# The S5 mixer of a recurrent decoder step: state operators by selection products on TensorE in place of products on VectorE and GpSimd

## The chip, the cores and the metric

The kernel runs on one core of a Trainium2 chip. The metric is the device time of one execution in microseconds (us); lower is better. The engines are TensorE (PE in the profile, its weight loads PEld), VectorE (DVE), ScalarE (ACT), GpSimd (POOL) and SyncE (SP, which here only issues DMAs).

## What is computed

One step of a decoder trunk on 592 tokens (16 meta tokens and a prompt of 512, then 8 running sequences of 8 tokens each), all in float32: an S5 layer, a causal convolutional feed-forward (ConvFFN), an RG-LRU layer, a second ConvFFN, each with a residual and a layer norm. The change is in the S5 layer. It projects x (592 x 1024) to u, runs 64 groups of 16 channels through a diagonal complex state space of 64 states a group, applies GELU, and multiplies by the output weights with a gate (GLU). For a group the recurrence is

```
A    = exp(step * lam)                  # 64 complex numbers
Bbar = (A - 1) / lam * B                # 64 x 16
h[t] = A * h[t-1] + Bbar u[t]
y[t] = 2 Re(C h[t]) + D u[t]            # gelu(y) goes on
```

The kernel does it in chunks of 8 tokens: 74 chunks (66 of the prompt, one a sequence). In a chunk, y is a Toeplitz product of u with the lag operators C A^d Bbar, d = 0 to 7; the state that a chunk adds is a product of u with A^j Bbar, j = 0 to 7; the states go from chunk to chunk by a scan; and what a chunk gets from earlier ones is a product of the state with C A^d, d = 1 to 8.

## The kernel before

Four pairs of groups make a **quad** (8 groups, one tile of 128 channels); there are eight quads. Every quad passes through these functions:

- project(m, h): half h of the tokens of channel tile m of u, 24 products (three for each k tile, L155 to L157: high and low parts of both factors); fetch_u brings u back by group and chunk through DRAM (DMA ud, u).
- fetch(q): one DMA (bc, L461) brings B and C of the quad, two steps ahead of their use.
- inputs(q, r): the operators A^j Bbar, real (r = 0) or imaginary, on VectorE: two products and a sum over 128x512 (L473 to L475). flip(q, r): their four transposes on TensorE (L483), a copy on ScalarE (L485), two small ones (L488).
- carries(q, r): C A^d by two products of 128x1024 on GpSimd (L509) and a sum on VectorE (L513); carry0 (L499) stacks C.
- lags(q): the lag operators on TensorE (L524). windows(q): ScalarE and VectorE put them into one tile (L530, L531), which a DMA writes to DRAM (td, L535). fetch_lags(q): reads them back in Toeplitz form (lagged, L539); toeplitz(q) reorders them on ScalarE (toe, L544).
- states(q): the states each chunk adds, 16 products (L563), then turned back by the angle of the chunk on VectorE (L567 to L570) and summed on GpSimd (L577, L578). decays (L551) makes the decay row. scans(q): the two scans (L587), four products (L588 to L593), and four quarter sums on GpSimd (L597). ends(q) saves and replaces the last states.
- phases(a), tables(a): angles (VectorE L436 to L445) and their cosines and sines (ScalarE L453) of two quads.
- outputs(q, h): for each group the Toeplitz product (L614) and the product with the state (L615) into one PSUM tile, GELU (L617), the write to DRAM (gd). fetch_gy and split_gy bring it back as the factor of the GLU.

The order of the work is written by hand under manual_schedule: each engine does its instructions in the order of the calls, and each DMA queue in the order of its issues. A step s runs the operators of quad s + 1, the states, lags and scans of quad s and the outputs of quad s - 1, with halves of projections between. Weights are streamed by load (wraw), split by convert_hi on ScalarE (whi, L126) and convert_lo (wlo, L135), which in the S5 stage stands on GpSimd. Behind the S5 stage the GLU, the feed-forwards and the RG-LRU follow; the change leaves them as they are.

## Time and profile before

| | us |
|---|---|
| three timed runs | 1405.79, 1408.65, 1410.70 |
| median | 1408.65 |
| span of the profiled execution (first to last instruction) | 1403.4 |
| its last product of an S5 output (line L615) ends at | 209.4 |
| TensorE busy over the span | 1310.7 |
| VectorE busy over the span | 897.2 |

The profiled execution is another one than the three timed; its span leaves out what lies before the first and behind the last instruction. TensorE carries the program; its granted clock has a mean of 0.964 of full speed over the span.

### The profile page before, as it was taken

Reading aid. Unit: us, or ns where it says so; the run is one execution under the profiler, and the core shown is the slowest. Engines: PE = TensorE matmul, PEld = TensorE weight load, DVE = VectorE, ACT = ScalarE, POOL = GpSimd, SP = SyncE. Lnnn points to the kernel's source line nnn. Section 1 sums busy time; section 2 is a strip of 40 time slices with the busy share of each in tenths; the row PEclk is TensorE's granted clock in tenths of the full one; section 3 lists DMA queues with packets and bytes.
Section 4 is the critical chain, followed back from the end, with each engine's and each line's share of the span. In section 5 each row is a group of like instructions: output and inputs, shape, how many; then the busy total and the mean of one; then the engine's idle time right before and its main releaser. Section 6 shows DMA issues by size and latency. Waiting matters only on the chain.

```text
span 1403.4 us, 23686 instructions
## 1 busy us (share of the span) xinstructions
PE 1310.7 (93%) x9708; PEld 1287.2 (92%) x9708; DVE 897.2 (64%) x1455; ACT 591.5 (42%) x950; POOL 385.7 (27%) x392
## 2 busy tenths in 40 slices
PE   5668889998999999999998999998999999999995
PEld 4667779998999999999998999998999999999994
DVE  8999996358655345535547989839755245535546
ACT  3654464235433134313334587734434133313433
POOL 5667753247000000000027521167200000000036
PEclk9888679999999999999999999999999999999998
DMA  6255454211222222222221212221322222222211
GB/s 200 63 154 163 133 152 173 90 61 55 96 90 76 82 84 72 79 91 76 82 81 61 81 55 94 80 84 57 109 91 76 91 76 87 70 101 78 80 52 68
DMA packets 70989, 127.80 MB, mean 91 GB/s; under 512 B 21216, under 2 KB 42848, under 8 KB 70880
## 3 DMA queue, kind: packets, MB, share of 16 engines
q1 hardware_dynamic: 61120, 120.71, 26.2%
q10 hardware_dynamic: 9760, 5.57, 1.4%
q8 instruction: 76, 1.25, 0.4%
q14 instruction: 33, 0.27, 0.1%
HBM read 113.61 MB, written 12.66 MB: 90 GB/s over the span
## 4 chain that ended last, share of the span: by engine, by line
PE 72%; DVE 21%; ACT 2%; issue 2%; DMA 1%; POOL 0%; SPq 0%; DVEq 0%; ACTq 0%
PE mm L157 23%; PE mm L156 23%; PE mm L155 23%; DVE wb L474 2%; DVE res L898 2%; DVE lo L904 1%; DVE wz L473 1%; DVE wz L475 1%; DVE wlo L135 1%; DVE res L870 1%; DVE t L587 1%; DMA wraw<-in_w5i 1%; PE y L615 1%; DVE ph L440 1%; PE y L614 1%
## 5 line engine op out<-in xcount | busy, mean ns | idle before, releaser
L156 PE MATMUL mm<-lo,whi 128*128 128x296 f32 (+2 forms) x2800 | 839.4, 300 | 20.8 <-DVE lo L904 10.4
L155 PE MATMUL mm<-hi,whi 128*128 128x296 f32 (+2 forms) x2800 | 841.2, 300 | 12.7 <-ACT whi L126 7.2
L157 PE MATMUL mm<-hi,wlo 128*128 128x296 f32 (+2 forms) x2800 | 837.8, 299 | 1.7 <-DVE wlo L135 1.7
L156 PEld LDWEIGHTS mm<-lo,whi 128*128 128x128 f32 x2800 | 532.2, 190 | 28.0 <-DVE lo L904 15.5
L155 PEld LDWEIGHTS mm<-hi,whi 128*128 128x128 f32 x2800 | 532.4, 190 | 15.9 <-ACT whi L126 7.2
L157 PEld LDWEIGHTS mm<-hi,wlo 128*128 128x128 f32 x2800 | 531.4, 190 | 2.5 <-DVE wlo L135 2.5
L135 DVE TENSOR_TENSOR wlo<-wraw,whi 128x1024 fp32r<-128x1024 f32 (+1 forms) x172 | 214.2, 1250 | 212.9 <-ACT whi L126 212.2
L126 ACT ACTIVATE whi<-wraw 128x1024 fp32r<-128x1024 f32 (+1 forms) x188 | 194.4, 1039 | 305.1 <-PE mm L156 298.0
L1088 POOL TENSOR_TENSOR tmp<-tmp,hist 128x16 f32<-128x16 f32 x88 | 20.4, 234 | 697.5 <-DVE tmp L1085 697.5
L1083 DVE SCALAR_TENSOR_TENSOR tmp<-mm,sm,tmp 128x512 f32<-128x512 f32 (+2 forms) x176 | 131.9, 750 | 0.0
L1087 ACT ACTIVATE stg<-mm 128x18 f32<-128x18 f32 x88 | 16.3, 185 | 185.7 <-DVE tmp L1085 185.7
L1135 DVE TENSOR_TENSOR res<-mm,res 128x296 f32<-128x296 f32 (+3 forms) x48 | 25.9, 558 | 81.2 <-PE mm L157 81.2
L1078 ACT ACTIVATE tmp<-mm,sm 128x592 f32<-128x592 f32 (+1 forms) x88 | 72.1, 822 | 0.0
L831 POOL TENSOR_TENSOR s<-s,res 128x296 f32<-128x296 f32 (+2 forms) x45 | 42.7, 951 | 62.0 <-DVE res L1039 31.5
L1094 DVE TENSOR_TENSOR tmp<-tmp 128x592 f32<-128x592 f32 (+1 forms) x44 | 33.7, 766 | 38.7 <-ACT tmp L1093 38.7
L172 DVE TENSOR_TENSOR lo<-tmp,hi 128x592 fp32r<-128x592 f32 (+2 forms) x48 | 36.6, 763 | 27.3 <-ACT hi L171 27.3
L171 ACT ACTIVATE hi<-tmp 128x592 fp32r<-128x592 f32 (+2 forms) x48 | 33.1, 690 | 42.7 <-DVE tmp L1094 30.0
L927 POOL TENSOR_SCALAR res<-res,sm 128x592 f32<-128x592 f32 (+1 forms) x24 | 49.1, 2063 | 7.0 <-DVE lo L904 7.0
L135 POOL TENSOR_TENSOR wlo<-wraw,whi 128x1024 fp32r<-128x1024 f32 x16 | 45.4, 2840 | 20.5 <-ACT whi L126 20.4
L614 PE MATMUL y<-u,toe 128*128 128x74 f32 x128 | 36.0, 379 | 15.8 <-ACT toe L544 15.8
L1133 DVE SCALAR_TENSOR_TENSOR res<-res,mm 128x592 f32<-128x592 f32 (+1 forms) x16 | 12.2, 762 | 59.2 <-PE mm L157 59.2
L832 POOL TENSOR_TENSOR s<-s,tmp 128x296 f32<-128x296 f32 (+2 forms) x53 | 49.5, 938 | 0.3 <-ACT tmp L827 0.3
(276 smaller groups left out, 1412.0 us busy)
## 6 DMA issues: line engine op xcount, KB each, us to landing
wraw<-in_wup SPq DMA_DIRECT2D x88, 512.0 KB, 3.2
wraw<-in_wdn SPq DMA_DIRECT2D x32, 448.0 KB, 3.3
wraw<-in_w5o SPq DMA_DIRECT2D x16, 512.0 KB, 4.3
wraw<-in_wdn SPq DMA_DIRECT2D x16, 512.0 KB, 3.4
wraw<-in_wri SPq DMA_DIRECT2D x16, 512.0 KB, 3.6
wraw<-in_w5i SPq DMA_DIRECT2D x8, 512.0 KB, 5.2
td<-lagsb SPq DMA_DIRECT2D x8, 512.0 KB, 3.3
lagged<-td SPq DMA_DIRECT2D x8, 512.0 KB, 3.8
```

Of the source, the lines that this page charges most:

```text
L126: A.activation(hi[:, 0:kk, :], t[:, 0:kk, :], AF.Copy)
L135: eng.tensor_tensor(lo[:, 0:kk, :], t[:, 0:kk, :], hi[:, 0:kk, :].bitcast(F32), op=ALU.subtract)
L155: T.matmul(out, hi[:, k, :], xh, start=start, stop=False)
L156: T.matmul(out, hi[:, k, :], xl, start=False, stop=False)
L157: T.matmul(out, lo[:, k, :], xh, start=False, stop=stop)
L172: V.tensor_tensor(lo[:, scols], src[:, scols], hi[:, scols].bitcast(F32), op=ALU.subtract)
L614: T.matmul(out, toe[:, g, :], u[:, g, :], start=True, stop=False)
L831: G.tensor_tensor(self.s1[:, cs_], RES[0][:, cs_] if m == 1 else self.s1[:, cs_], z, op=ALU.add)
L832: G.tensor_tensor(self.s2[:, cs_], self.s2[:, cs_], sq[:, cs_], op=ALU.add)
L927: G.tensor_scalar(z, z, bm, None, op0=ALU.add)
L1078: A.activation(acc[:, d0:NT], X(d0, NT), AF.Identity, scale=w[2], bias=fcb[:, l, m:m + 1])
L1083: V.scalar_tensor_tensor(acc[:, a:TP], X(a - sh, TP - sh), w[k], acc[:, a:TP], op0=ALU.mult, op1=ALU.add)
```

## The change

Of each operator, only small factors are kept, and TensorE spreads them out. Before the loop, bbar makes Bbar (128x16 a pair) and turn and turn_b transpose it and the powers of A (aT, bT). flip_b(q) then multiplies Bbar by a constant selection matrix of zeros and ones, so that it comes out repeated for each j, transposed (eight products on halves of the rows), and ScalarE copies it to bt three times (real, imaginary, negated). operators(q) spreads the powers in the same way (eight products on quarters of the rows), and VectorE multiplies the two in two instructions of 128x1024 (xw). The sums and differences of the complex products are left to PSUM: states has 32 products in place of 16, outputs 32 products with v on halves of the rows in place of 8 on all, and lags 16 in the second group in place of 8. carries makes v by four products of 128x512 on GpSimd, without a sum. Real and imaginary parts lie side by side, so that scans and turned work on both in one instruction of 128x592. The reordering toe is gone: outputs reads lagged itself, and fetch_gy restores the order of channels, by eight DMAs in place of one. All lower halves of weights are on VectorE. C is fetched by fetch_c in front of assemble, its one reader; three projections in place of two stand ahead of the first states.

```diff
-PROJ = (1, 3, 2, 2, 1, 1, 2)     # halves of projections beside the steps
-TABLES = {1: (3,)}
-PJ0 = 2           # projections ahead of the first states
+PJ0 = 3
...
+            def bbar(a0, a1):
+                n = a1 - a0
+                shape = [P, n, NQ, 16]
+                t = wide()
+                t1, t2 = (t[:, i, 0:64 * n].rearrange("p (q i h) -> p q i h", q=n, h=16) for i in range(2))
+                qv = [v[:, NQ * a0:NQ * a1].rearrange("p (q i) -> p q i", i=NQ)[:, :, :, None].to_broadcast(shape)
+                      for v in (qr, qi)]
+                br, bi = (bB[:, a0:a1, a].rearrange("p q (i h) -> p q i h", h=16) for a in range(2))
+                for (a, b, op), r in zip(((br, bi, ALU.subtract), (bi, br, ALU.add)), range(2)):
+                    V.tensor_tensor(t1, a, qv[0], op=ALU.mult)
+                    V.tensor_tensor(t2, b, qv[1], op=ALU.mult)
+                    V.tensor_tensor(bb[:, a0:a1, r], t1, t2, op=op)
...
+            def fetch_c(q):
+                CC[q] = s5.tile([P, 256], F32, tag="bc", name="bc", bufs=2)
+                nc.sync.dma_start(CC[q], s5bc[q, :, 128:384])
+            def assemble(q):
+                cc = CC[q].rearrange("p (a i g h) -> p a i g h", a=2, g=2, h=16)
+                c = s5.tile([P, 2, NQ, 16], F32, tag="cq", name="cq", bufs=2)
+                bst = bsts[q % 2]
+                for g in range(2):
+                    rows = slice(64 * g, 64 * g + 64)
+                    A.activation(c[rows, 0], cc[rows, g, :, g, :], AF.Copy)
+                    A.activation(c[rows, 1], cc[rows, 1 - g, :, g, :], AF.Copy, scale=-1.0)
+                    for r in range(2):
+                        A.activation(bst[rows, r, :, 16 * g:16 * g + 16], bb[rows, q, r], AF.Copy)
+                CC[q] = c
...
-            def inputs(q, r):
-                V.tensor_tensor(w, xr, f[r], op=ALU.mult)
-                V.tensor_tensor(t2, xi, f[1 - r], op=ALU.mult)
-                V.tensor_tensor(w, w, t2, op=ALU.add if r else ALU.subtract)
...
+            def flip_b(q):
+                BT[q] = s5.tile([P, 3, NQ * P], F32, tag="bt", name="bt")
+                pt = [sp.tile([P, 512], F32, tag="tr", name="tr", bufs=2) for _ in range(2)]
                 for i in range(NQ):
+                    for r in range(2):
+                        rows = slice(64 * r, 64 * r + 64)
+                        T.matmul(pt[r][:, i * P:(i + 1) * P], sel_b[rows, i].rearrange("p h j -> p (h j)"),
+                                 bT[rows, q, :], start=True, stop=True)
+                A.activation(BT[q][:, 0], pt[0], AF.Copy)
+                A.activation(BT[q][:, 1], pt[1], AF.Copy)
+                A.activation(BT[q][:, 2], pt[1], AF.Copy, scale=-1.0)
+            def operators(q):
+                b3 = BT.pop(q)
+                XW[q] = s5.tile([P, 2, 2, NQ * P], F32, tag="xw", name="xw")
+                pt = [sp.tile([P, 512], F32, tag="tr", name="tr", bufs=2) for _ in range(2)]
+                for i in range(NQ):
+                    for r in range(2):
+                        rows = slice(32 * (q % 2 * 2 + r), 32 * (q % 2 * 2 + r) + 32)
+                        T.matmul(pt[r][:, i * P:(i + 1) * P], sel_a[rows, i].rearrange("p h j -> p (h j)"),
+                                 aT[rows, q // 2, :], start=True, stop=True)
+                for r, part in enumerate((b3[:, 0:2], b3[:, 0:3:2])):
+                    V.tensor_tensor(XW[q][:, r], part, pt[r][:, None, :].to_broadcast([P, 2, NQ * P]), op=ALU.mult)
...
-                    G.tensor_tensor(t, cc[:, r, :, :, None].to_broadcast(vsh), f, op=ALU.mult)
-                V.tensor_tensor(v, v, BST.pop(q), op=ALU.add)
+            def carries(q):
+                c = CC[q]
+                VV[q] = v = s5.tile([P, 4, NQ, CH, 16], F32, tag="v", name="v", bufs=2)
+                sh = [P, NQ, CH, 16]
+                for m, (a, b) in enumerate(((0, apr), (1, api), (0, nai), (1, apr))):
+                    G.tensor_tensor(v[:, m], c[:, a, :, None, :].to_broadcast(sh),
+                                    b[:, NQ * q:NQ * q + NQ, 1:CH + 1, None].to_broadcast(sh), op=ALU.mult)
...
+                v, c, bst = VV[q], CC.pop(q), bsts[q % 2]
                 pl = sp.tile([P, 512], F32, tag="tr", name="tr", bufs=2)
+                for n in range(2):
+                    for i in range(NQ):
+                        T.matmul(pl[32 * i:32 * i + 32, 0:16], bst[:, n, i, :], c[:, n, i, :], start=n == 0, stop=n == 1)
+                for n in range(4):
+                    for i in range(NQ):
+                        T.matmul(pl[32 * i:32 * i + 32, 16:P], bst[:, n // 2, i, :],
+                                 v[:, n, i, 0:CH - 1, :].rearrange("p d h -> p (d h)"), start=n == 0, stop=n == 3)
...
-            def toeplitz(q):
-                toe = s5.tile([P, NG, P], F32, tag="toe", name="toe", bufs=2)
-                A.activation(toe.rearrange("p g (h j) -> p g h j", j=CH),
-                             TOE[q].rearrange("p g j h -> p g h j"), AF.Copy)
-                TOE[q] = toe
...
+            def states(q):
+                u, x_ = U[q], XW.pop(q)
+                pb = []
+                for n, terms in (("br", (x_[:, 0, 0], x_[:, 1, 1])), ("bi", (x_[:, 1, 0], x_[:, 0, 1]))):
+                    ps = sp.tile([P, 512], F32, tag=n, name=n, bufs=1)
+                    for i in range(NQ):
+                        for t, w in enumerate(terms):
+                            for g in range(2):
+                                T.matmul(ps[64 * g:64 * g + 64, NK * i:NK * i + NK],
+                                         w[:, P * i + 64 * g:P * i + 64 * g + 64], u[:, 2 * i + g, :],
+                                         start=t == 0, stop=t == 1)
+                    pb.append(ps[:, 0:HALF])
+                ST[q] = pb
+            both = [P, 2, HALF]
+            def scans(q):
+                cs_ = RES[q].rearrange("p (a t) -> p a t", a=2)
+                a, b = (v[:, None, :].to_broadcast(both) for v in ST.pop(q))
+                m1, m2 = wide(), wide()
+                V.tensor_tensor(m1, a, cs_, op=ALU.mult)
+                V.tensor_tensor(m2, b, cs_, op=ALU.mult)
+                V.tensor_tensor(m1[:, 0], m1[:, 0], m2[:, 1], op=ALU.add)
+                V.tensor_tensor(m1[:, 1], m2[:, 0], m1[:, 1], op=ALU.subtract)
+                v = m1.rearrange("p a (q k) -> p a q k", q=NQ)[:, :, :, KP:NK]
+                V.tensor_tensor(v, v, sm8[:, :, NQ * q:NQ * q + NQ, :], op=ALU.add)
+                d0 = D0.pop(q).rearrange("p q k -> p (q k)")
+                for r in range(2):
+                    V.tensor_tensor_scan(m1[:, r], d0, m1[:, r], 0.0, ALU.mult, ALU.add)
+                ST[q] = m1, m2
+            def turned(q):
+                cs_ = RES[q].rearrange("p (a t) -> p a t", a=2)
+                m1, m2 = ST.pop(q)
+                m3 = wide()
+                V.tensor_tensor(m2, m1[:, 0:1].to_broadcast(both), cs_, op=ALU.mult)
+                V.tensor_tensor(m3, m1[:, 1:2].to_broadcast(both), cs_, op=ALU.mult)
+                sx = sxt[q % 2]
+                quad = lambda t: t.rearrange("p (q k) -> p q k", q=NQ)
+                V.tensor_tensor(sx[:, 0, :, 1:NK + 1], quad(m2[:, 0]), quad(m3[:, 1]), op=ALU.subtract)
+                V.tensor_tensor(sx[:, 1, :, 1:NK + 1], quad(m2[:, 1]), quad(m3[:, 0]), op=ALU.add)
...
+                ps = [sp.tile([P, 512], F32, tag="y", name="y", bufs=2) for _ in range(2)]
+                at_ = lambda g, i: ps[g][:, NK * i:NK * i + NK]
+                for g in range(2):
+                    for i in range(NQ):
+                        T.matmul(at_(g, i), toe[:, 2 * i + g, :], u[:, 2 * i + g, :], start=i == 0, stop=False,
+                                 skip_group_check=True)
                 for i in range(NQ):
+                    for m in range(4):
                         for g in range(2):
+                            rows = slice(64 * g, 64 * g + 64)
+                            T.matmul(at_(g, i), v[rows, m, i].rearrange("p d h -> p (d h)"), sx[rows, m // 2, i, 0:NK],
+                                     start=False, stop=m == 3, skip_group_check=True)
...
-                nc.sync.dma_start(RES[q], GD.pop(q))
+                gd = by_group(GD.pop(q)).rearrange("(j h) g k -> g h j k", j=CH)
+                for g in range(NG):
+                    nc.sync.dma_start(RES[q][16 * g:16 * g + 16, :].rearrange("p (j k) -> p j k", j=CH), gd[g])
...
+                for s in range(DM):
+                    last = s == DM - 1
+                    run(fetch_gy, s - 2)
+                    run(fetch_u, s + 1)
+                    states(s)
+                    scans(s)
+                    if last:
+                        lags(s)
+                        windows(s)
+                        fetch_lags(s)
+                    else:
+                        operators(s + 1)
+                        project_next()
+                    run(ends, s - 1)
+                    run(outputs, s - 1)
+                    turned(s)
+                    run(carries, s + 1)
+                    if not last:
+                        lags(s)
+                        windows(s)
+                        fetch_lags(s)
+                        decays(s + 1)
+                    run(fetch_c, s + 2)
+                    run(assemble, s + 2)
+                    run(flip_b, s + 2)
+                    project_next()
+                    more_weights()
                        if s == 0:
                         phases(2)
                         tables(2)
+                        bbar(5, 8)
+                        turn_b(5, 8)
+                        phases(3)
+                        tables(3)
...
```

Two places show the new order. The first is SyncE, which issues the DMAs, in one step of the middle (td, lagged: the lag operators' way out and back; bc: the fetch of B and C or of C; u, res: the fetches of u and of the outputs). Before:

```order
L626 DMA res_70<-gd_1510 128x592
L461 DMA bc<-in_s5bc 128x384
L430 DMA u<-ud_1451 128x8x74
L535 DMA td_1635<-lagsb 1024x1x128
L539 DMA lagged<-td_1635 128x8x128
```

And now:

```order
L641 DMA res_70<-gd_1764 16x8x74 x8
L439 DMA u<-ud_1616 128x8x74
L551 DMA td_2015<-lagsb 1024x1x128
L555 DMA lagged<-td_2015 128x8x128
L468 DMA bc<-in_s5bc 128x256
```

The fetch bc has moved from ahead of the pair td, lagged to behind it.

The second is ScalarE in the same stretch, from the copy of the lags on (d: the decay row; cq, bst: the small operands of the lags; bt, wt: the flipped input operands; tr: a PSUM tile). Before:

```order
L530 ACTIVATE lagsb<-tr 128x112
L499 ACTIVATE c_1476<-bc 64x128 x2
L551 ACTIVATE d_1479<-sp_347,sp_341 128x74 x4
L617 ACTIVATE gu<-y 128x296 x2
L623 DMA gd_1510<-gu 128x8x74
L485 ACTIVATE wt<-tr 128x512
```

And now:

```order
L546 ACTIVATE lagsb<-tr 128x112
L561 ACTIVATE d_1317<-sp_324 128x296
L477 ACTIVATE cq<-bc 64x64
L478 ACTIVATE cq<-bc 64x64
L480 ACTIVATE bst_125<-bb 64x4x16 x2
L477 ACTIVATE cq<-bc 64x64
L478 ACTIVATE cq<-bc 64x64
L480 ACTIVATE bst_125<-bb 64x4x16 x2
L504 ACTIVATE bt<-tr 128x512
L505 ACTIVATE bt<-tr 128x512
L506 ACTIVATE bt<-tr 128x512
```

The readers of bc now stand directly ahead of the three copies that empty the PSUM tiles tr; before, GELU and the copies of the flipped operators came behind copies of a bc that another step had fetched.

## Rows read from the trace of the kernel before

**Rows 1.** The page, 40 slices of the span: busy tenths of VectorE; granted TensorE clock.

```profile
DVE  8999996358655345535547989839755245535546
PEclk9888679999999999999999999999999999999998
```

**Rows 2.** Windows: stretch, length, busy (count) PE PEld DVE ACT POOL, clock, DMA, GB/s.

```profile
0.00:209.40 209.40, 153.57 (x1241) 141.26 (x1241) 201.26 (x341) 108.36 (x220) 137.05 (x101) 0.80 0.48 143
210.00:300.00 90.00, 90.00 (x664) 90.00 (x663) 40.33 (x91) 31.29 (x49) 24.49 (x28) 1.00 0.33 116
```

**Rows 3.** Groups by line, 0 to 209.4 us, VectorE: busy, mean ns, idle before.

```profile
L474 DVE TENSOR_TENSOR wb<-bc,sp 128x512 f32<-128x512 f32 x16 | 34.1, 2134 | 0.0
...
L475 DVE TENSOR_TENSOR wz<-wz,wb 128x512 f32<-128x512 f32 x16 | 25.3, 1580 | 0.5
L473 DVE TENSOR_TENSOR wz<-bc,sp 128x512 f32<-128x512 f32 x16 | 20.6, 1288 | 0.0
...
L440 DVE CUSTOM_DVE_ANT_0 ph<-ph 128x32 uint16<-128x32 uint16 (+5 forms) x28 | 14.6, 522 | 0.7
```

**Rows 4.** Groups by line, the same stretch, GpSimd and ScalarE.

```profile
L597 POOL TENSOR_TENSOR sx<-t 64x296 f32<-64x296 f32 x30 | 33.3, 1111 | 26.8 <-DVE t L589 24.8 <-DVE t L593 0.4
...
L135 POOL TENSOR_TENSOR wlo<-wraw,whi 128x1024 fp32r<-128x1024 f32 x9 | 28.1, 3119 | 12.5 <-ACT whi L126 12.4
...
L509 POOL TENSOR_TENSOR v<-bc,sp 128x1024 f32<-128x1024 f32 x8 | 19.9, 2489 | 0.4
L544 ACT ACTIVATE toe<-lagged 128x1024 f32<-128x1024 f32 x8 | 15.6, 1950 | 0.4 <-ACT gu L617 0.4
...
L485 ACT ACTIVATE wt<-tr 128x512 f32<-128x512 f32 x16 | 9.4, 591 | 16.3 <-PE tr L483 15.8 <-ACT gu L617 0.5
```

**Rows 5.** Timeline, TensorE: start, duration, line, operation, count [idle before, releaser].

```profile
45.96 1.25 PE L563 MATMUL br<-u,wt 128*64 128x74 f32 x16 [0.78 <-ACT wt L485]
...
191.39 0.30 PE L157 MATMUL mm<-hi,wlo 128*128 128x296 f32 x1
191.62 0.73 PE L563 MATMUL br<-u,wt 128*64 128x74 f32 x16
192.19 0.68 PE L563 MATMUL bi<-u,wt 128*64 128x74 f32 x16
```

**Rows 6.** Timeline, TensorE, output products.

```profile
124.09 0.39 PE L615 MATMUL y<-sx,v 128*128 128x74 f32 x2
124.31 0.39 PE L614 MATMUL y<-u,toe 128*128 128x74 f32 x2
```

**Rows 7.** Timeline, TensorE, behind two waits.

```profile
132.77 1.09 PE L483 MATMUL tr<-ident,wz 128*128 128x128 f32 x4 [4.73 <-DVE t L586]
...
142.43 0.49 PE L614 MATMUL y<-u,toe 128*128 128x74 f32 x2 [1.90 <-ACT toe L544]
```

**Rows 8.** Timeline, TensorE, lags of a quad.

```profile
139.39 0.32 PE L524 MATMUL tr<-c,bst 128*32 128x16 f32 x16
139.54 1.00 PE L524 MATMUL tr<-v,bst 128*32 128x112 f32 x16
```

**Rows 9.** Timeline, SyncE: issue of td and of lagged in one step.

```profile
108.47 0.53 SPq L535 DMA_DIRECT2D td<-lagsb  x1
111.82 0.38 SPq L539 DMA_DIRECT2D lagged<-td  x1
```

**Rows 10.** DMA: lagged (median us to landing), and least, median, most of the tile bc.

```profile
lagged<-td SPq DMA_DIRECT2D x8, 512.0 KB, 3.8
...
DMA to landing us min/median/max: 3.3/4.1/5.2
```

**Rows 11.** Timeline, ScalarE: the two small copies of C.

```profile
124.11 0.61 ACT L499 ACTIVATE c<-bc 64x128 f32<-64x128 f32 x2
```

**Rows 12.** Windows, TensorE alone, behind the waits of rows 7: clock, DMA share, GB/s last.

```profile
132.50:135.90 3.40, 3.13 (x36) 0.50 0.91 302
142.70:152.90 10.20, 10.20 (x70) 0.50 0.56 164
```

More of the change, by code (lines that the diff above doesn't have):

```diff
@@ new lines, in trunk @@
+                operators(0)
+                fetch_u(0)
+                assemble(0)
+                carries(0)
+                flip_b(1)
+                assemble(1)
+                decays(0)
+                G.tensor_tensor(sm8[:, 0], sp1[:, 0], m8b, op=ALU.mult)
+                G.tensor_tensor(sm8[:, 1], sp1[:, 1], m8b, op=ALU.mult)
+                phases(1)
+                tables(1)
+                bbar(2, 5)
+                turn_b(2, 5)
+                for s in range(DM):
[25 more added lines that the diff above has]
+                    more_weights()
+                    if s == 0:
@@ L720, in trunk @@
-                    run(outputs, s - 1, 1)
-                    if s == -1:
-                        tables(1)
-                    else:
-                        flip(s + 1, 0)
-                        flip(s + 1, 1)
-                        scans(s)
-                    for p in halves[1:]:
-                        project(*p)
-                    if s > -1:
-                        carries(s + 1, 2)
-                    for a in TABLES.get(s, ()):
-                        phases(a)
-                        tables(a)
@@ L779, in trunk @@
+                    if last:
+                        convert_lo(12)
+                        split_gy(4)
+                        residual(0, 2)
+                a, b = DM - 2, DM - 1
+                fetch_gy(a)
                 ends(b)
-                split_gy(4)
+                outputs(b)
+                load(15)
                 split_gy(5)
-                outputs(b, 0)
-                outputs(b, 1)
-                glu_part(0, 0, 6)
-                convert_hi(12)
-                convert_lo(12)
@@ L787, in trunk @@
-                fetch_gy(a)
                 residual(2, 4)
+                glu_part(0, 0, 6, False)
+                split_gy(a)
                 fetch_gy(b)
-                load(15)
+                st = s5.tile([P, NP, 2, 9], F32, tag="gu", name="st", bufs=2)
+                for r in range(2):
+                    for g in range(2):
+                        A.activation(st[64 * r:64 * r + 64, :, g, :], hold[64 * g:64 * g + 64, :, r, :], AF.Copy)
+                nc.sync.dma_start(o_s5, st.rearrange("p n g s -> p (n g) s"))
```

404 lines of the change are left out of this document (116 added, 288 removed).

## The prediction

> **What bounds the kernel now.** I read the page's slices first: VectorE is at nine tenths in the first six of forty slices and never so dense again, and the clock row is low there and at its top afterwards [rows 1]. That stretch is the S5 mixer. A table by stretches fixes its end: until 209.4 us VectorE is busy 201.26 of 209.40 us, TensorE 153.57 at a mean clock of 0.80; behind it TensorE is busy 90.00 of 90.00 us at 1.00 [rows 2]. So the stage is bounded by VectorE, the rest by TensorE, and the diff leaves the rest's work alone. The span is 1403.4 us, the median of the three timed runs 1408.65, so 5.25 us lie outside the span; I add the change of the stage's end to the median. About 0.3% (4.2 us) is what a measurement of this kernel can tell from no change.
>
> Next come the groups by line in the stage. VectorE's operator products and sums L473 to L475 cost 20.6 + 34.1 + 25.3 = 80.0 us [rows 3]. All of it goes, and the sum L513 too. GpSimd's four quarter sums L597 (33.3 us) and ScalarE's reordering L544 (15.6 us) go too [rows 4]; the lower halves of the weights, nine at 3.1 us on GpSimd (L135), come to VectorE. VectorE gets besides two products of 128x1024 a quad for the operators, and the scan's products at double width. Even at GpSimd's price for the lower halves it stays well below what it gave up. This is the change's promise. What it costs must be looked for on TensorE and in the new order.
>
> **TensorE's own work after the change, at full clock.** Prices per call; one call in fp32 is two instructions in the trace.
> - States, 32 calls of 64 columns a quad: 16 instructions took 0.57 us from start to start at full clock [rows 5], so 64 take 2.3 us (before 1.15).
> - Output products: the y calls follow each other every 0.22 us [rows 6]. Eight of them with the lag operators make 1.8 us. The carried part becomes 32 calls on halves of the rows; no row shows a row tile. Bounds: two at a time (16 x 0.22 = 3.6 us) and one by one (32 x 0.22 = 7.1 us); below the first, at the price of the column tiles of rows 5, 64 x 0.036 = 2.3 us. I take 4.2, near the half, since the column tiles do overlap.
> - Selection products: eight for the operators, eight for the flip. Four transposes of the same size took 1.09 us at the low clock behind a wait [rows 7], so 0.55 at the full one: 1.1 us for eight one by one, 0.55 in pairs. I take 0.9 for each eight. They replace the eight transposes of before.
> - Lags: 16 small ones, 0.15, and twice the former second group of 1.00 [rows 8]: 2.1 us.
> - A quad is 2.3 + 1.8 + 4.2 + 1.8 + 2.1 = 12.2 us; eight are 97.6, less 2.7 for what of quads 0 and 1 stands ahead of the first states. Five projections are left (three go ahead, one more than before): 240 products each 0.136 us apart, as the 664 in 90 us are [rows 2], 32.5 us. GLU products in the stage: 36, 4.9 us. Sum 132 us.
> The head (x, the parameters, the first projections) trades one more projection and the small operands' turns against two rounds of large products; before, the first states start at 45.96 us [rows 5], beside a VectorE that is at nine tenths [rows 1]; with one projection more (6.5 us), partly hidden, I put them at about 50. Were TensorE never to wait after that, the stage would end at 182.
>
> The Trainium skill, TensorEngine Tiling (Array Packing), Key Properties, says that different tiles load weights and multiply in parallel: by it the carried part is 3.6 us a quad and the sum 5 us less; one by one it would be 23 us more. The column tiles of rows 5 agree; no row here shows a row tile. The same section says that a change of tiling mode drains TensorE, which speaks against so many short groups. In row terms the step from projections to states is 0.23 us where products are 0.14 apart, so 0.1 us for a change: three more a quad would be 2 us in all, and I leave them in the rounding.
>
> **The waits that the new order makes.** Call T the end of a step's lags on TensorE. In the printed orders SyncE issues the window write (td), then waits for its landing, issues the read (lagged), and only then the fetch of C for the quad after next (bc), which stood ahead of td before. From td's issue to lagged's issue is 3.35 us [rows 9]; td is issued some 0.6 behind T, bc's issue is 0.5 behind lagged's, and bc lands in 4.1 (3.3 at best) [rows 10]: T + 8.5. On ScalarE the eight small copies of assemble wait for it: about 0.3 us each by the pair at 124.11 [rows 11], 2.5 us. Behind them stand the three copies of the flipped operands, 0.5 apart (0.59 each, L485 [rows 4]). They free the two PSUM tiles that the next operators() needs: T + 12.5. TensorE comes there by itself at T + 7: flip 0.9, half a projection 3.3, states 2.3, with the change of clock a little more. So it waits about 5 us in each of the five steps that have such a fetch behind them: **25 us**. Hidden until now, because bc was asked for a whole step ahead; that cover is gone.
>
> Step 0 has more. The lower half of a weight on VectorE waits for the upper one on ScalarE, which stands behind those same copies; behind it VectorE makes phases(2) (seven additions L440 of 0.52, a copy, a sum: about 6 us [rows 3]) and bbar(5,8) (six short ones, 3 us at L440's price). TensorE's turn_b(5,8) needs these, and states(1) stands behind turn_b. So states(1) come at about T + 24 instead of T + 7: **17 us**.
>
> At the end, step 7 puts states and lags together, and outputs(6), outputs(7) each wait for a landing (lagged, 3.8 us [rows 10] behind 3.35 + 0.5) and for VectorE's scans: about 2 us three times, plus 2 for gated halves that wait on ScalarE in steps 5 and 6: **8 us**.
>
> **Clock.** After TensorE's wait of 4.73 us at 132.77 the granted clock reads 0.50 over 3.4 us; the stretch from 142.7, behind a wait of 1.90, is at 0.50 for 10.2 us [rows 7, 12]. That is the lower level, 1.2 GHz. Seven new waits of 5 us and more should each leave such a stretch. It costs half its length, 1.7 to 5.1 us; I take 3, seven times: **21 us**. (Before pays this also, but its TensorE had slack under VectorE.)
>
> **Tail.** split_gy(5) is put behind the last gelu on ScalarE and gated products wait for it; fetch_gy becomes eight DMAs in place of one, 0.38 to 0.53 us an issue by rows like those of [rows 9], some 3.5 us for all. About **4 us**.
>
> **What moves at no cost.** The removed work on VectorE, GpSimd and ScalarE leaves the path as soon as TensorE and the fetch chain set the step; GpSimd's four products of 512 columns for v (1.25 us each by L509's 2.5 for 1024 [rows 4], 5 us a quad) lie beside a step of over 20 us; the lower weights on VectorE beyond step 0 lie in its idle time.
>
> Sum: 182 + 17 + 25 + 8 + 21 = 253 us for the stage's end, 209.4 before: +44, with the tail +48. **1408.65 + 48 = 1457 us.**
>
> **Rivals.**
> 1. *The chain is hidden (faster).* If from the end of the lags to the third copy it takes under 7 us, TensorE never waits at operators(), the clock stays up, step 0's wait shrinks by the same 5 us: 182 + 12 + 8 = 202, with the tail 1405; and with row tiles at the column tiles' price (32 x 0.036 x 2 = 2.3 in place of 4.2, selections at 0.55) 20 us less: 1385. Middle 1393. For it: VectorE loses 80 us and more, and TensorE's own way would end at 182. Against: two landings and one issue stand in a row ahead of the copies, 3.35 + 0.5 + 3.3 alone are over 7 us [rows 9, 10]. Chance 0.10.
> 2. *Row tiles run one by one, and TensorE stays at 0.50 through the outputs.* The carried part 7.1 (+23 in all), selections at 1.1 (+3), low stretches of 10 us (+14): 1457 + 40 = 1497. For it: y bursts that began low stayed low for 10.2 us [rows 12]; no row shows a row tile. Chance 0.20.
> 3. *No difference.* Waits of 3 us in place of 5, step 0 at 10, half the low stretches, row tiles at the column tiles' price: 253 - 10 - 7 - 11 - 15 = 210, the tail hidden beside the GLU's first products: 1409. VectorE's freed time and the longer TensorE step cancel. Chance 0.10, of which half falls within 0.3%.
>
> **Numbers.** The forecast as argued has 0.60 and its own range 1430 to 1480. It takes up the bounds of the unknown prices (row tiles -15 to +23, waits -10 to 0, clock -9 to +15). With rival 3 and half of 2 the range that should hold it 8 times in 10 is 1410 to 1494. Chance of faster by over 0.3%: rival 1, 0.10; within 0.3%: 0.05; slower: 0.85.
>
> **What would show it.** Right: the stage's end near 253 instead of 209.4; VectorE's share in the stage down to about 0.6; TensorE's waits led by the selection products L516, released by the copies L504 to L506 of bt, and those copies and L477 in turn behind a landing of bc; a gap of over 10 us at step 0 ahead of L487 or L575; the clock at 0.50 after each. The carried products L629 tell the price of row tiles by their spacing (0.11 or 0.22 us a call). Wrong: a stage that ends before 205 us, TensorE that waits for VectorE's products instead, or bc landing before TensorE comes to L516.

## The result and the profile after

The changed kernel takes **1474.33 us** (median of four runs, 1474.19 to 1479.01), the kernel before 1408.63 on the same chip: ratio 1.047, 95% interval 1.045 to 1.0491. It is 66 us slower; 1457 was forecast, 1410 to 1494 the range. The profiled execution is the slowest of the four (1479.01, its span 1477.2), so its sums lie some 5 us above the median. One execution of the early fetch of C took 2186.28 us at a mean granted clock of 0.554 and is left out below (with it, that run's median is 1430.0).

The last S5 output product ends at 280.2 us, where it ended at 209.4. The slices and the windows of the stage, which answer to [rows 1, 2] (same columns):

```profile
DVE  7642425363875534553454788975855435544546
...
PEclk9778876799999999999999999999999999999998
```

```profile
106.70:133.10 26.40, 21.75 (x274) 20.28 (x274) 9.79 (x15) 6.53 (x21) 4.27 (x7) 0.87 0.44 112
133.10:159.70 26.60, 21.88 (x272) 20.51 (x272) 9.79 (x15) 6.44 (x20) 4.17 (x7) 0.87 0.42 111
0.00:280.20 280.20, 197.68 (x2213) 182.11 (x2213) 134.16 (x308) 83.75 (x209) 44.38 (x77) 0.78 0.39 109
```

VectorE fell from 201.26 to 134.16 us, ScalarE from 108.36 to 83.75, GpSimd from 137.05 to 44.38. TensorE's busy time rose from 153.57 to 197.68, and no engine is busy all of the time any more: in the two steps shown, of 26.4 and 26.6 us, TensorE idles 4.7 us of each and runs at a mean clock of 0.87. What the stage waits for, by TensorE's waits (line, releaser: us in total, times, longest):

```profile
PE tr L516 <- ACT bt L504: 19.1, 5, 6.2
PE mm L153 <- ACT hi L655: 13.4, 2, 11.4
PE tr L487 <- DVE ph L445: 13.2, 1, 13.2
PE tr L487 <- DVE bb L401: 9.8, 1, 9.8
PE mm L153 <- ACT whi L124: 6.9, 1, 6.9
PE y L623 <- DMA lagged<-td: 5.0, 1, 5.0
PE tr L502 <- DVE lagsb L547: 3.5, 5, 1.9
```

The first line is the forecast wait at the selection products: four times in steps 2 to 5, 3.8 to 6.2 us each, and once in the head, 0.7. The third is step 0's transposes, behind phases and bbar. The second (the splits for the gated products in steps 5 and 6) and the fourth (the head) were not foreseen at this size. One of the four waits in full, on the timelines of SyncE, ScalarE and TensorE (columns as in [rows 7]):

```profile
133.05 0.53 SPq L551 DMA_DIRECT2D td<-lagsb  x1
137.01 0.39 SPq L555 DMA_DIRECT2D lagged<-td  x1
137.45 0.57 SPq L468 DMA_DIRECT2D bc<-in_s5bc  x1
```

```profile
141.67 0.26 ACT L477 ACTIVATE cq<-bc 64x64 f32<-64x64 f32 x1 [8.58 <-DMA bc<-in_s5bc]
...
143.08 0.60 ACT L504 ACTIVATE bt<-tr 128x512 f32<-128x512 f32 x1
143.58 0.59 ACT L505 ACTIVATE bt<-tr 128x512 f32<-128x512 f32 x1
144.05 0.60 ACT L506 ACTIVATE bt<-tr 128x512 f32<-128x512 f32 x1
```

```profile
138.70 1.20 PE L575 MATMUL bi<-u,xw 128*64 128x74 f32 x32
143.73 0.48 PE L516 MATMUL tr<-aT,sel 32*128 32x128 f32 x2 [3.84 <-ACT bt L504]
144.71 1.91 PE L516 MATMUL tr<-aT,sel 32*128 32x128 f32 x14 [0.49 <-ACT bt L506]
```

This is the chain as it was written down: td issued, lagged 3.96 us later (3.35 in [rows 9]), bc 0.44 behind it, its landing 4.2 behind the issue, 1.4 us of small copies (2.5 had been taken), three copies 0.5 apart. TensorE has been done with the states since 139.9.

### The profile page after: what moved, and what is told of

The parts are those of the page before. It is cut to its first block, busy times and chain, and to the rows that moved or that the text cites. A ratio compares the mean times of both kernels' runs of the same rounds, so it can differ in the third digit from the quotient of the medians.

```text
span 1477.2 us, 25646 instructions
## 1 busy us (share of the span) xinstructions
PE 1357.8 (92%) x10680; PEld 1330.8 (90%) x10680; DVE 828.5 (56%) x1421; ACT 568.0 (38%) x942; POOL 292.7 (20%) x368
## 3 DMA queue, kind: packets, MB, share of 16 engines
q1 hardware_dynamic: 70224, 120.46, 26.4%
## 4 chain that ended last, share of the span: by engine, by line
PE 75%; DVE 13%; DMA 5%; ACT 4%; issue 2%; POOL 1%; SPq 0%; ACTq 0%; DVEq 0%
PE mm L155 23%; PE mm L154 23%; PE mm L153 23%; PE y L629 2%; DMA td<-lagsb 2%; DMA bc<-in_s5bc 2%; DVE res L869 1%; DVE lo L875 1%; PE y L623 1%; DVE wlo L133 1%; DVE res L841 1%; PE tr L516 1%; PE br L575 1%; DVE tmp L847 0%; DVE tmp L1237 0%
## 5 line engine op out<-in xcount | busy, mean ns | idle before, releaser
L153 PE MATMUL mm<-hi,whi 128*128 128x296 f32 (+2 forms) x2800 | 844.6, 302 | 26.2 <-ACT hi L655 13.4
L133 DVE TENSOR_TENSOR wlo<-wraw,whi 128x1024 fp32r<-128x1024 f32 (+1 forms) x181 | 225.8, 1253 | 262.0 <-ACT whi L124 261.2
L527 POOL TENSOR_TENSOR v<-cq,ap 128x512 f32<-128x512 f32 x32 | 34.9, 1120 | 192.8 <-PE y L629 153.9
L798 ACT ACTIVATE tmp<-res 128x296 f32<-128x296 f32 (+2 forms) x56 | 24.0, 444 | 60.5 <-DVE res L1106 24.7
L1056 DVE SCALAR_TENSOR_TENSOR tmp<-mm,sm,tmp 128x56 f32<-128x56 f32 (+1 forms) x176 | 46.3, 263 | 0.0
```

What stands on the lines that cost most here:

```text
L133: eng.tensor_tensor(lo[:, 0:kk, :], t[:, 0:kk, :], hi[:, 0:kk, :].bitcast(F32), op=ALU.subtract)
L153: T.matmul(out, hi[:, k, :], xh, start=start, stop=False)
L1056: V.scalar_tensor_tensor(sa[:, :, sh:8], sx[:, :, 0:8 - sh], w[k], sa[:, :, sh:8], op0=ALU.mult, op1=ALU.add)
```

## The experiments

Each edit is against the changed kernel unless it says otherwise.

**The fetch alone.** One line moves to the head of the step.

```diff
+                    run(fetch_c, s + 2)
                     run(fetch_gy, s - 2)
...
-                    run(fetch_c, s + 2)
                     run(assemble, s + 2)
```

> The changed kernel with one line moved: the fetch of C for the quad after next is issued at the head of the step, ahead of td and lagged. Theory A (the serial chain td, lagged, bc, small copies, bt copies sets TensorE's wait at the selection products): the waits at L516, 20.9 us in the profile after, go to under 4; the gated products' wait of 11.4 us in step 5, which stands behind the same copies, shrinks by some 8; the low clock behind each wait gives back about 2 us five times. Together 30 to 40 us less: 1435 to 1445. Theory B (TensorE's own longer work sets the step, a wait that goes comes back as the next one): under 10 us less, 1465 to 1474.

1428.88 us, ratio to the kernel before 1.0139 (1.0102 to 1.0176): 45 us less than the change, more than the 30 to 40 of theory A. In the trace the wait at L516 shrinks from 20.9 us in all (L504 and L506 together) to 1.2, all of it in the head; the wait of step 0 goes from 13.2 to 8.2 and the splits' wait from 13.4 to 4.5. The windows of the same two steps read:

```profile
99.00:117.60 18.60, 18.25 (x272) 17.25 (x272) 9.77 (x15) 6.43 (x22) 4.16 (x7) 1.00 0.60 158
117.60:136.40 18.80, 18.33 (x274) 17.32 (x274) 9.81 (x16) 6.57 (x22) 4.30 (x7) 1.00 0.61 159
```

A step takes 18.7 us instead of 26.5, with the same instructions, at a clock of 1.00: 7.8 us a step, where the wait itself was 4.3 (3.84 + 0.49). The other 3.5 are the clock: a mean of 0.87 over 26.5 us makes 3.4 us lost to the lower level.

**The reverse move in the kernel before.**

```diff
-                    fetch(s + 2)
...
                     run(fetch_lags, s)
+                    fetch(s + 2)
```

> The kernel before with its fetch of B and C put behind td and lagged, as the change has it. Its readers stand a step later, so theory A (only a reader directly behind the fetch makes the wait) says no difference: 1404 to 1413. Theory C (the place on the queue costs by itself, by transfers that meet td, lagged and the weights there): 1415 or more.

1409.0 us, ratio 1.0001 (0.9988 to 1.0014). There, where the readers of bc stand a step later, the place in the queue costs nothing. With the early fetch this says what costs in the change: a reader, and behind it the copies that free TensorE's PSUM tiles, directly behind the fetch.

**The gap filled with products that nobody reads.** In steps 1 to 5:

```diff
+                            w, t = UT[s + 2][0], sp.tile([P, 512], F32, tag="y", name="y", bufs=2)
+                            for k in range(DM):
+                                mm3(t[:, 0:HALF], w, k, HX[k][0][:, 0:HALF], HX[k][1][:, 0:HALF], k == 0, k == DM - 1)
                         operators(s + 1)
```

> The changed kernel with work added: in steps 1 to 5 a half projection is done once more, into a PSUM tile that nobody reads, in the place where TensorE waits for the bt copies. It changes no result. The added products take 3.25 us at full clock in a gap of about 4. Theory D (the gap costs twice: as a wait, and by the low clock behind it): the selection products, the projection and what follows run at full clock, a step falls from 26.5 to some 24, the whole to about 1462. Theory E (the low clock does not come from the gap, or does not matter): no gain, 1472 to 1482.

1469.48 us (ratio 1.0434, 1.041 to 1.0457): 5 us less than the change, with 120 products more; the two intervals just overlap. The windows of three steps (TensorE alone: stretch, length, busy, clock, DMA share, GB/s):

```profile
107.50:132.30 24.80, 22.27 (x298) 1.00 0.52 130
132.30:156.00 23.70, 23.30 (x298) 0.93 0.42 114
156.00:181.70 25.70, 23.81 (x296) 0.93 0.47 115
```

The first two are the steps that took 26.4 and 26.6 us at 0.87, the third took 28.3 (159.72 to 188.04). They got shorter with more work in them, so part of what the gap cost was the low clock behind it, as theory D says; of its 12 us the medians show 5. The profiled execution here is the fastest of its four (1463.92), that of the change the slowest of its own, so the windows show the mechanism better than its size.

**The preparations spread over the steps**, in order to remove the waits of 9.8 and 13.2 us:

```diff
-                phases(1)
-                tables(1)
-                bbar(2, 5)
-                turn_b(2, 5)
...
                         operators(s + 1)
+                        if s in (0, 2):
+                            bbar(*((2, 5) if s == 0 else (5, 8)))
...
                     run(assemble, s + 2)
+                    if s in (0, 2):
+                        turn_b(*((2, 5) if s == 0 else (5, 8)))
```

> The changed kernel with the preparations taken apart: bbar(2,5) with its transposes from ahead of the first states into step 0, bbar(5,8) into step 2, phases and tables of quads 2 and 3, 4 and 5, 6 and 7 to the ends of steps 0, 1, 3. Theory A (TensorE stands in order behind transposes that VectorE feeds late): the waits of 9.8 us ahead of the first states and 13.2 us in step 0 go, some 20 us less, 1450 to 1460. Theory B (VectorE's work is only put off and is met again at scans and operators): 1468 to 1476.

1480.99 us (1.051, 1.0488 to 1.0533): 7 us worse. The waits went where the edit put them:

```profile
PE tr L502 <- ACT bB L489: 22.1, 2, 13.1
```

The copy behind turn_b now stood on ScalarE behind assemble, and so behind the landing of bc. This is the forecast chain once more, met by another instruction. The time lies outside both ranges, so the run decides nothing between A and B.

> Both edits together. Theory A: the two add up, 50 to 60 us less than the changed kernel, 1414 to 1426, still above the kernel before by what TensorE's longer work and the low clock cost. Theory B: not below 1455.

With the early fetch this trap is gone, and the sum is 1429.72 (1.0153, 1.0136 to 1.0171), the same as the early fetch alone and in neither range. VectorE's preparations came back as waits inside the first steps (6.1 us at L487 for bbar, 9.8 at the flips for the windows). So the spread itself gained nothing, as theory B has it, but B's "not below 1455" fell with the gain of the fetch.

**The head, into time in which VectorE idles.** In the trace of the early fetch, VectorE stands idle ahead of the first operators (timeline of VectorE):

```profile
41.92 2.35 DVE L519 TENSOR_TENSOR xw<-bt,tr 128x1024 f32<-128x1024 f32 x2 [9.83 <-PE tr L516]
```

Into these 9.83 us go bbar and phases(1), on top of the early fetch; the transposes then need not wait (shown in part: tables(0) also moves ahead of turn_b(0, 2), and the old places in step 0 go):

```diff
                 flip_b(0)
+                bbar(2, 5)
+                bbar(5, 8)
+                phases(1)
                 operators(0)
...
-                phases(1)
                 tables(1)
-                bbar(2, 5)
                 turn_b(2, 5)
+                turn_b(5, 8)
...
+                    if s == 0:
+                        phases(2)
                     run(flip_b, s + 2)
+                    if s == 0:
+                        tables(2)
+                        phases(3)
```

> The early fetch of C (1430 by itself) and the preparations moved into time in which VectorE idles: bbar(2,5), bbar(5,8) and phases(1) ahead of operators(0), where VectorE waits 9.8 us for TensorE; all transposes of Bbar ahead of the first states; phases of quads 4 to 7 behind the windows of step 0, ahead of the weights. Theory A: the waits of 8.3 and 8.2 us at the transposes L487 go, step 0 falls from 31 to about 20 us: 1408 to 1414. Theory B (as the spread showed, work put elsewhere on VectorE comes back as another wait): 1424 or more.

1416.04 us (1.0059, 1.0045 to 1.0072): 13 us less than the early fetch alone, 2 above theory A's range and clear of B's. The waits at L487 for VectorE are gone; td of steps 0 and 1 is issued at 62.43 and 83.61, 21.2 us apart, where it was 31.0. What decides is which idle time takes the work up; GpSimd, too, stands idle until 42.41 here, which the last section comes back to.

**The end.** First attempt, on the early fetch: the splits and gated products of steps 5 to 7 stand behind operators, and in step 7 behind the lags.

```diff
                         operators(s + 1)
                         project_next()
+                    if s == 5:
+                        split_gy(0)
+                        convert_hi(10)
+                        convert_lo(10)
+                        split_gy(1)
+                        glu_part(0, 0, 2, False)
...
+                    if last:
+                        split_gy(3)
+                        glu_part(0, 0, 4, False)
                     run(ends, s - 1)
```

> The early fetch of C and another order of the last three steps: the gated products and their splits stand in the gap behind the selection products instead of behind the flips, in step 7 behind the lags, and lags of the last quad come ahead of them. Theory A: the waits for the splits (4.5 and 3.2 us) and for the last lagged (5.0) shrink, and the outputs behind them run at full clock (5.7 instead of 10.8 us): 10 to 18 us below the early fetch alone, 1412 to 1420. Theory F (the tail behind the last GELU sets the end, whatever stands before): 1425 to 1432.

1439.93 us (1.0242, 1.0216 to 1.0268), 11 worse than the early fetch alone and above both ranges; with the head in addition:

> All three: early fetch, head, end. Theory A: they add up to 1390 to 1402, under the kernel before (1408.5). Theory B or F: 1408 or more.

1429.09 us (1.015, 1.0129 to 1.0171), 13 worse than the head without it, in the range of theories B and F. The low parts stood on VectorE behind scans and operators, and the products waited 5.50 us for them. Second attempt, with the head, and the splits ahead of the scans (shown in part: the split of quad 5 also moves ahead of the last outputs):

```diff
                     states(s)
+                    if s == 5:
+                        split_gy(0)
+                        convert_hi(10)
+                        convert_lo(10)
+                        split_gy(1)
+                    if s == 6:
+                        split_gy(2)
+                        split_gy(3)
+                    if last:
+                        split_gy(4)
                     scans(s)
...
                         windows(s)
+                        fetch_gy(s - 2)
                         fetch_lags(s)
...
+                    if s > 4:
+                        glu_part(0, 0, 2 * s - 8 if s < 7 else 5, False)
                     run(ends, s - 1)
```

> Early fetch of C, the head as in the run before, and the last three steps once more: the splits for the gated products now stand ahead of the scans on VectorE (in the attempt before, the low part waited 5.5 us behind scans and operators), the fetch of the outputs of quad 5 behind the last td instead of ahead of it, the split of quad 5 and its gated products ahead of the last outputs. Theory A (the end's waits are a matter of places in the queues): steps 5 and 6 fall from 21 and 24 us to 18 or 19, the last outputs run at full clock: 15 to 25 us under the early fetch with the head (1416), 1391 to 1401, clear of the kernel before. Theory F (the tail behind the last GELU sets the end): 1412 or more.

1414.18 us (1.0033, 1.0017 to 1.0048), 2 us less than without, which the intervals don't tell apart, and in theory F's range. The long waits for the splits in steps 5 and 6 are gone, the time is not. TensorE in steps 5 and 7 of that kernel:

```profile
147.21 0.41 PE L153 MATMUL mm<-hi,whi 128*128 128x296 f32 x1 [0.35 <-ACT hi L655]
148.56 0.61 PE L154 MATMUL mm<-lo,whi 128*128 128x296 f32 x1 [0.94 <-DVE lo L656]
150.70 3.53 PE L623 MATMUL y<-u,lagged 128*128 128x74 f32 x16
154.15 7.11 PE L629 MATMUL y<-sx,v 64*128 64x74 f32 x64
...
189.52 3.67 PE L623 MATMUL y<-u,lagged 128*128 128x74 f32 x16 [4.71 <-DMA lagged<-td]
193.12 7.11 PE L629 MATMUL y<-sx,v 64*128 64x74 f32 x64
```

Two waits that add to 1.29 us are followed by 10.6 us of outputs at the low clock, which take 5.6 at the full one. Four of the twelve executions lie at 1407.79 to 1409.27 us, with a mean granted clock of 0.976 or 0.977, the other eight at 1412.90 to 1416.92 with 0.963 to 0.970; the trace is of one of the eight.

With GpSimd as the issuer of the eight small fetches, on top of the second attempt:

```diff
-                    nc.sync.dma_start(RES[q][16 * g:16 * g + 16, :]
+                    nc.gpsimd.dma_start(RES[q][16 * g:16 * g + 16, :]
```

> The same with the eight small fetches of each quad's outputs issued on GpSimd instead of SyncE, where they hold the queue for 4 to 8 us a step in the profile after. If that hold is on the path (u, td or lagged wait behind it): 3 to 8 us less than the same kernel without. If not: within 3 us, or slower where GpSimd's own products for v come late.

1418.77 us (1.0079, 1.0063 to 1.0095): 4.6 us more than with SyncE, nothing gained. In the steps of the middle the hold of SyncE was not on the path: td of steps 1 and 2 are 18.65 us apart, 18.66 with SyncE. What made it slower was not looked into.

**Products that nobody reads, in the end's gaps.** On top of the second attempt, a helper that issues n products of 296 columns into a free PSUM tile:

```diff
+            def idle(n, tag, w, pairs):
+                t = sp.tile([P, 512], F32, tag=tag, name=tag, bufs=2)
+                for i in range(n):
+                    T.matmul(t[:, 0:HALF], w[0][:, i % 8, :], pairs[i % len(pairs)][0][:, 0:HALF], start=True, stop=True)
...
                     run(ends, s - 1)
+                    if last:
+                        idle(36, "tr", GW[0][0], GY[0:4])
                     run(outputs, s - 1)
```

> The run before last (1414) with products that nobody reads put where TensorE waits in the last three steps: 12, 8 and 4 ahead of the gated products of steps 5, 6, 7, 36 ahead of the outputs of quad 6 (a wait of 4.7 us for lagged), 22 ahead of the gated products before the last outputs (3.0). No result changes. In the trace before, three of the last four output blocks run at the low clock behind such waits, 10.7 us each in place of 5.7. Theory D (the low clock behind a wait is what keeps the end long): the blocks take 5.7 us, the S5 stage ends some 12 to 16 us earlier, 1396 to 1404, under the kernel before. Theory F (landing of lagged and the outputs' way through DRAM set the end, whatever the clock): the stage ends within 4 us of before, 1410 or more.

1404.08 us, ratio to the kernel before 0.9968 (0.9955 to 0.9982). The same two blocks:

```profile
151.34 1.90 PE L623 MATMUL y<-u,lagged 128*128 128x74 f32 x16
153.17 3.80 PE L629 MATMUL y<-sx,v 64*128 64x74 f32 x64
...
186.78 1.90 PE L623 MATMUL y<-u,lagged 128*128 128x74 f32 x16
188.61 3.80 PE L629 MATMUL y<-sx,v 64*128 64x74 f32 x64
```

82 added products bring 10 us, and all twelve executions lie below the fastest of the second attempt. The last S5 output product ends at 203.15, where it ended at 216.42: 13.3 us earlier, in theory D's range, so F falls. What stands behind it became 3.0 us longer, with the waits that the last run is about.

Last, the fetch of the last outputs:

```diff
                 load(15)
+                fetch_gy(b)
                 residual(2, 4)
                 split_gy(a)
-                fetch_gy(b)
```

> The run before (1404) with one more move: the fetch of the last quad's outputs is issued ahead of two fetches of the residual, which hold SyncE for 8 us behind the last GELU. In its trace TensorE waits 2.5 + 0.6 us in the GLU for that quad's split, at a granted clock of 0.93 there. If the hold of the queue is on the path: 3 to 5 us less, 1399 to 1401. If the landing comes no earlier (the transfers share the DMA engines anyway) or other waits follow: 1403 to 1406.

1399.87 us, ratio 0.9939 (0.9922 to 0.9956): 4 us less, as expected, though the two intervals just touch; behind the last S5 output product the trace is 4.4 us shorter (1195.4 for 1199.8), and the wait of 2.5 us is gone. **This version is under both kernels**: 74 us under the change as it was made, 9.7 (0.6%) under the kernel before. It holds the change's arithmetic; only orders and products without a reader differ.

## Why the prediction was right, and where its sum was off

The direction and the range held, the forecast's own 1430 to 1480 too, and the chain behind the late fetch is what the one-line move shows. The sum was 17 us short, and no more than that by luck, since terms that came out too large took up part of what was missing. Its stage end is 253, in the profiled execution 280.2. From the first states on:

```profile
58.92:280.20 221.28, 162.91 (x2013) 150.67 (x2012) 91.05 (x148) 54.77 (x145) 26.73 (x38) 0.77 0.37 97
```

| | forecast | profiled execution |
|---|---|---|
| first states at | 50 | 58.9 |
| TensorE's work at full clock | 132 | 125 (estimate) |
| TensorE idle | 17 + 25 + 8 = 50 | 58.4 (221.28 - 162.91) |
| lost to the low clock | 21 | 37 (estimate) |

The last row takes the mean clock of 0.77 for the busy time (0.23 of 162.91 us), the second what is then left of it. So the largest miss is the clock; then come the waits at the end and the head, below. TensorE's work, step 0 and the waits at the selection products came out smaller than their terms. The stage's 27 us are 17 in the medians mostly since the profiled execution of the change is its slowest and that of the kernel before a quick one (a span of 1403.4, where others of it have up to 1408.9): in each of the four executions of the change time and span differ by 1.8 us, so of the 5.25 us that the prediction puts outside the span most is a difference between two executions. No term rests on it. By the steps of the sum:

- **TensorE's own work.** The carried part takes 3.7 us a quad at full clock, 4.2 taken, close to the bound of 3.6 for two at a time. The lags, put at 2.1 us a quad by doubling a group of before, take 1.0 (131.16 to 132.19):

```profile
127.43 3.80 PE L629 MATMUL y<-sx,v 64*128 64x74 f32 x64
131.16 0.32 PE L536 MATMUL tr<-cq,bst 128*32 128x16 f32 x16
131.30 0.95 PE L539 MATMUL tr<-v,bst 128*32 128x112 f32 x32
132.19 0.48 PE L502 MATMUL tr<-bB,sel 64*128 64x128 f32 x2
...
205.92 7.11 PE L629 MATMUL y<-sx,v 64*128 64x74 f32 x64
212.97 0.41 PE L536 MATMUL tr<-cq,bst 128*32 128x16 f32 x16
```

 64 instructions on row tiles in 3.73 us (0.058 each) stand against 16 on the full array in 1.83 (0.114 each), so two row tiles at a time. The Trainium skill, TensorEngine Tiling (Array Packing), Key Properties, says that different tiles can load weights and multiply in parallel; the trace agrees. The selection products were mis-sized: eight take 1.1 us, not 0.9,

```profile
94.79 1.16 PE L516 MATMUL tr<-aT,sel 32*128 32x128 f32 x16
```

 as 16 instructions of 0.07 us, where the transposes that gave the price are one instruction each [rows 7]. At the low clock the carried part takes 7.05 us (the last two lines of the block that begins at 127.43).
- **Waits at the selection products.** 25 us forecast as five waits of 5. There are four in steps 2 to 5, 19.7 us in all, 4.9 each; the other 1.2 of the 20.9 lie in the head. The chain is right, its small copies 1.1 us shorter than their price.
- **Step 0.** 17 forecast, 13.2 measured, at the place named and by the chain named. VectorE, the releaser by name, itself stood idle for 13.12 us, for the upper half of a weight that ScalarE made behind the copies that wait for bc (timelines of ScalarE and VectorE):

```profile
79.75 0.26 ACT L477 ACTIVATE cq<-bc 64x64 f32<-64x64 f32 x1 [10.03 <-DMA bc<-in_s5bc]
83.45 1.06 ACT L124 ACTIVATE whi<-wraw 128x1024 fp32r<-128x1024 f32 x1 [0.40 <-ACT ut L432]
84.53 1.23 DVE L133 TENSOR_TENSOR wlo<-wraw,whi 128x1024 fp32r<-128x1024 f32 x1 [13.12 <-ACT whi L124]
```

 Its phases(2) and bbar(5,8) then took 5.0 us (85.68 to 90.64), where the prediction's prices of the kernel before made 9.
- **The head** is a step that failed: first states at 50, in fact at 58.92 (timeline of TensorE, where [rows 5] have 45.96 for the kernel before):

```profile
58.12 0.87 PE L487 MATMUL tr<-ident,bb 128*128 128x128 f32 x3 [9.84 <-DVE bb L401]
58.92 2.24 PE L575 MATMUL br<-u,xw 128*64 128x74 f32 x32
```

 A wait of 9.8 us for bbar(2,5) on VectorE stands ahead of them. The sum had taken the head as nearly equal and priced only its projection, and put this wait at nothing; the order of the changed kernel held that turn_b(2,5) stands ahead of states(0) and phases(1) ahead of bbar(2,5).
- **The end.** 8 us forecast, 21.6 measured (13.4 + 3.2 for the gated products' splits and 5.0 for lagged). The splits on ScalarE stand behind the same bt copies, so in step 5 the chain of the fetch was paid once more, 11.4 us long, where the sum had 2 for both steps. With that, each of the six fetches of C was paid once: in step 0, at four selection products and here.
- **Clock.** 3 us a wait taken, seven times. In the two windows shown it is 3.4 a step, and the early fetch takes it away with the wait; but over the stage some 37 were lost, not 21. This term failed by its size. Behind a wait in step 5 and one behind step 7 whole output blocks run at the low level: 10.7 us from 202.30 and from 269.46, where 5.6 are enough at the full one.
- **Rivals.** That the chain is hidden fell: TensorE waited behind each of the six fetches. But it is what the one-line move makes true, and then the step is TensorE's own 18.7 us. Of rival 2 one half fell (row tiles run one by one), the other came true in part: two of the eight output blocks stayed at the low clock, and the clock's excess of 16 us is near the 14 that it gave. That nothing differs fell. VectorE's share is 0.48 (0.6 expected); its own work stood on TensorE's path in the head and in step 0.

With the early fetch and the head, 8 us over the kernel before are left (1416). The last three edits that stayed took 16 us off at the end of the stage and behind it. So TensorE's longer work does not keep the change above the kernel as it stood before. That the change is worth something by itself is not shown: without the products that nobody reads its best version is 0.3% slower than the kernel before, and the kernel before was not given such products nor the earlier fetch of the last outputs.

## What to carry to other kernels

When work leaves the engine that bounded a stage, the next bound need not be another engine's work; here it was the place of one fetch. Look at each fetch whose reader moves, and ask what stands in order behind the reader. A wait on TensorE is priced with the low clock behind it, here 4.3 us of wait and 3.5 of clock. Ask also which long blocks come behind the wait: the output blocks that began low here stayed low and cost 5 us each. Put displaced work into idle time that the trace shows, on an engine whose next instruction isn't waited for; a place that only looks free moves the wait.

## What the runs showed of the hardware that was not expected

In the second attempt at the end the clock was low behind waits much shorter than those of the change: in step 5, waits of 0.35 and 0.94 us were followed by 10.6 us of outputs at the low clock, and with 12 products without a reader in their place the same block took 5.6. Not every short wait did this: in step 6 of the second attempt waits of 0.35 and 0.47 us left the clock at 0.99 (165 to 185 us).

VectorE's unchanged instructions became faster as GpSimd emptied. The additions of phases, against [rows 3], by line in the stage after:

```profile
L449 DVE CUSTOM_DVE_ANT_0 ph<-ph 128x32 uint16<-128x32 uint16 (+5 forms) x28 | 8.9, 318 | 0.7
```

318 ns each, 522 before, with GpSimd busy 44.38 us of the stage instead of 137.05. The trace after has the same comparison within itself: phases(1) with bbar(2,5) in the head, and the same 16 instructions as phases(2) with bbar(5,8) in step 0 (windows, columns as in [rows 2]):

```profile
46.07:57.97 11.90, 2.07 (x14) 1.78 (x14) 11.52 (x17) 7.24 (x25) 10.71 (x12) 0.50 0.00 1
85.68:90.64 4.96, 0.00 (x0) 0.00 (x0) 4.58 (x18) 2.61 (x4) 0.00 (x0) 0.50 0.00 0
```

Beside a busy GpSimd they take 11.9 us, beside an idle one 5.0; that difference of 6.9 us is most of the head's miss. In the run of the head they stand ahead of GpSimd's products, and phases(1) takes 3.0 us there (35.94 to 38.9) instead of 5.9. That GpSimd's activity is the cause was not tried by itself. The Trainium skill, SBUF — State Buffer, Who interferes with whom, says that a VectorE instruction with two inputs in SBUF contends with a GpSimd instruction that reads SBUF; the additions and GpSimd's products for v are such instructions, and the trace agrees.
